# A two-block transformer kernel on one core: first tokens multiplied during the norm of the second, tokens stationary in the first block after each norm and in the gated layers, eight weight halves, the root in a diagonal tile

## The chip, the cores and the metric

The kernel runs on one core of one Trainium2 chip. The metric is device time in microseconds, the median of three runs: 1670.88 (1669.81 to 1671.94).

## The reference, cut to what matters

256 tokens of width 1024 pass through two blocks, everything in 32-bit floats. Each stage begins with an RMS norm over the whole width, so its first product needs the finished rows:

```python
h = h + concat(attn, rec) @ w_out            # after proj = rmsnorm(h) @ w_in      (mix1)
h = rmsnorm(h + peer(rmsnorm(h, norm2_g)))   # 2048-wide queries, top-16 keys, 16384 experts
# second block, two layers (even, odd), sh/sc/g from c @ ada_w + ada_b
hm = modulate(rms_norm(x, mix_norm), sh_m, sc_m)
x  = x + g_m * (mixer(hm) @ w_out)           # even: convolutions and a gated recurrence; odd: attention
hf = modulate(rms_norm(x, ffn_norm), sh_f, sc_f)
x  = x + g_f * ((silu(hf @ w_gate) * (hf @ w_up)) @ w_down)     # 2816 hidden columns
```

There are six norms that feed a product: before mix1, peer, even, the gated layer of even (here ffn0), odd, and the gated layer of odd (ffn1). The norm that closes the first block and the one that opens even are done in one pass.

## The kernel before, in words

Tokens lie in two groups of 128 (t = 0 and 1). Precision is kept by writing every operand as a sum of two parts, hi and lo; each product is three matmuls (hi hi, lo hi, hi lo).

**Weights** come as a stream of 1 MB units (`stream_init`, `load`, `unit`). One unit is fetched into one of two raw buffers by a DMA on SP's queue, and each of its halves (128 x 1024) is split: ScalarE (ACT) copies hi (L163), VectorE (DVE) subtracts lo (L166; some units on GpSimd). There are three buffers of halves (`SPB`, L364), and `unit` loads one unit ahead (`LA`, L149).

**Products** take two forms. `wstat` (L186) has the weights stationary and 256 token columns moving: 24 matmuls for 128 output columns, the output lies with columns on partitions. `xstat` (L200) has 128 tokens stationary and 512 weight columns moving. `out_n` (L218) uses it for products 1024 wide, with four accumulators [t][c] in PSUM; the last three steps of k (`TAIL`) are ordered by t and column group, so the first tokens end first. `out_n512` (L237) is the same for 512 columns, both token groups in turn.

**A norm** (`norm_t`, L304) runs per token group: add the four accumulators of the stage before to the residual (`add_res`, with a gate row multiplied in where there is one), squares (half on ACT, half on DVE), a root by Newton steps on DVE (`rsqrt1`, eight instructions on one column), scaling of the row by it (L332, L334), eight transposes on TensorE (PE, L338), gain and shift per column (L345 to L352, half on ACT, half on DVE), and the split of the result into hi and lo (L355, L356). The stage's first `wstat` needs both token groups.

**Gate rows** (`grow`, L949) lay a modulation column out along the free axis: 8 diagonal tiles on DVE, 8 fp32 matmuls with ones (16 instructions), two copies. The modulation itself (`ada_steps`) is 48 steps on DVE per layer, spread over pv and over even with ffn0.

**Order.** A planner lays out each engine's queue in advance: the program's order is the priority, an instruction that the planner's cost table does not hold for ready is passed by later ones, and `issue_after` pins one behind another on its engine. At run time each queue is in order.

The gated layer (`ffn`, L964) takes 22 steps, each with two `wstat` (gate, up), a Silu on ACT, a multiply on DVE and the split of the result. Names of the stages by their weights: wp and wo (mix1), wq, pu, pv (peer), wi0, wo0, fgu0, fd0, wi1, wo1, fgu1, fd1.

Of the kernel before, what the change touches and what calls it, by code (L numbers as in the profile page):

```python
# [18 lines left out]
D = 1024  # L19
# [69 lines left out]
def layout(i):  # L89
# [6 lines left out]
        _wcols(w, 2048, 4), _wcols(w, 1536, 4), qk[0:2], _wrows(w, 1024, 512),  # L96
        qk[2:4], _wrows(w, 2560, 512), _wrows(w, 3072, 512)], axis=0)
    a["wo"] = _wrows(g("w_out")[0])
    a["wq"] = _wcols(g("peer_wq")[0], 0, 16)
# [5 lines left out]
    for l in "01":  # L105
        a["ada" + l] = g(f"l{l}_ada_w_2").T.reshape(48, 128, 1024)
        a["fgu" + l] = _wpair(g(f"l{l}_ffn_w_gate_2"), g(f"l{l}_ffn_w_up_2"), 0, 0, 22)
# [3 lines left out]
    a["wi0"] = np.concatenate([_wcols(w, 2048, 4), _wcols(w, 512, 8), _wcols(w, 0, 4), _wcols(w, 1536, 4)], axis=0)  # L111
# [23 lines left out]
class Prog:  # L135
# [4 lines left out]
    def stream_init(self):  # L140
        order = []
        for nm in ("wp", "wo", "wq", "pu", "pv", "wi0", "wo0", "fgu0", "fd0", "wi1", "wo1", "fgu1", "fd1"):
            order.extend((nm, j) for j in range(self.i[nm].shape[0]))
# [5 lines left out]
    LA = 1  # L149

    POOLED = {"wq": (2, 8), "pu": (0, 6)}

    def load(self, n):
# [5 lines left out]
        for h in range(2):  # L159
            s = r[:, h * 1024:(h + 1) * 1024]  # L160
            hi = self.wp.tile([128, 1024], F32R, name="hi", bufs=self.SPB)
            lo = self.wp.tile([128, 1024], F32R, name="lo", bufs=self.SPB)
            nc.scalar.copy(hi, s)  # L163
            a, b = self.POOLED.get(nm, (0, 0))
            eng = nc.gpsimd if a <= j < b else nc.vector
            ins = eng.tensor_tensor(lo, s, hi.bitcast(F32), op=ALU.subtract)  # L166
# [19 lines left out]
    def wstat(self, half, x, K=8):  # L186
# [4 lines left out]
        pt = self.pt([128, 256])  # L191
        for k in range(K):
            c = slice(k * 128, k * 128 + 128)
            nc.tensor.matmul(pt, hi[:, c], xh[:, k], start=k == 0, stop=False)  # L194
            nc.tensor.matmul(pt, hi[:, c], xl[:, k], start=False, stop=False)  # L195
        for k in range(K):
            nc.tensor.matmul(pt, lo[:, k * 128:k * 128 + 128], xh[:, k], start=False, stop=k == K - 1)  # L197
        return pt

    def xstat(self, acc, half, x, k, first, last, cg, ts=(0, 1)):  # L200
# [3 lines left out]
        for t in ts:  # L204
# [4 lines left out]
            for c, cs in cg:  # L209
# [3 lines left out]
                nc.tensor.matmul(a, xl, hi[:, cs], start=False, stop=last)  # L213

    TAIL = 3
# [21 lines left out]
    def out_n512(self, nm, j0, x, lead=0, step=None):  # L237

        acc = [[self.acc([128, 512])] for t in range(2)]
        us = []  # L240

        def part(k, t):
# [3 lines left out]
            self.xstat(acc, us[k // 4][k // 2 % 2], x, k, k == 0, k == 7, [(0, slice(o, o + 512))], ts=(t,))  # L246

        for k in range(8 + lead):
            if k < 8:
                part(k, 0)  # L250
            if k >= lead:
                part(k - lead, 1)
# [1013 lines left out]
```

## Time and profile before

| | us |
|---|---|
| median of the runs | 1670.88 |
| the profiled execution | 1669.5 |
| its span | 1667.4 |
| PE busy | 1588.8 |
| DVE busy | 1272.1 |
| ACT busy | 863.0 |
| mean granted TensorE clock | 0.981 |

A matmul's shown duration holds its latency; what one costs in a stream is the distance from one start to the next. "x8" is eight instructions merged into one row. A wait is put down to the releaser that came last. In the windows the share of the clock is that of 2.4 GHz, so 0.5 is the lower of its two levels.

### The profile page before, as it was taken

To read this page: it belongs to the slowest core of one execution; us is meant where nothing else is said; L and a number is where in the kernel's file an instruction comes from. 1 tells how busy PE (TensorE), PEld (TensorE's weight loads), DVE (VectorE), ACT (ScalarE), POOL (GpSimd) and SP (SyncE) were. 2 spreads that over 40 slices of the span, in tenths; PEclk is the share of its full clock that TensorE was granted. 3 is DMA by queue.
4 is the path that set the end of the run, shared out by engine and by line. 5 is a ranking of instruction groups with operands and counts; after the bars stand their busy time and mean duration, and the time that the engine had idled before them with its cause. 6 is when DMAs were issued, how large, how long until landed. Compare 5 with 4: busy or idle time off the path is not lost.

```text
span 1667.4 us, 27542 instructions
## 1 busy us (share of the span) xinstructions
PE 1588.8 (95%) x10454; PEld 1448.1 (87%) x10454; DVE 1272.1 (76%) x2944; ACT 863.0 (52%) x1515; POOL 86.1 (5%) x47
## 2 busy tenths in 40 slices
PE   6998998999999999999999996989999799979998
PEld 6886898999999999888888886979998687779997
DVE  6967489868889897787777788967887877665544
ACT  6544445445444444555555555645444467654442
POOL 0310462000000000000000000000000000000000
PEclk9999899999999999999999998999999899989999
DMA  5324343544444444877777774656888453235554
GB/s 206 127 102 152 132 172 127 203 169 143 147 149 153 152 153 162 285 284 262 260 273 261 273 261 156 219 181 237 324 317 296 165 184 116 87 116 188 177 180 149
DMA packets 52405, 320.97 MB, mean 192 GB/s; under 512 B 5808, under 2 KB 6192, under 8 KB 20144
## 3 DMA queue, kind: packets, MB, share of 16 engines
q1 hardware_dynamic: 51264, 315.75, 53.8%
q10 hardware_dynamic: 1008, 3.47, 0.6%
q8 instruction: 81, 1.33, 0.3%
q14 instruction: 52, 0.43, 0.1%
HBM read 318.15 MB, written 1.05 MB: 191 GB/s over the span
## 4 chain that ended last, share of the span: by engine, by line
PE 88%; DVE 8%; ACT 1%; DMA 1%; issue 1%; POOL 0%; DVEq 0%; ACTq 0%
PE pt L194 15%; PE pt L195 15%; PE pt L197 15%; PE acc L211 12%; PE acc L212 12%; PE acc L213 12%; PE acc L829 3%; DVE lo L166 2%; PE pt L491 1%; PE pt L338 1%; PE pt L1166 1%; ACT hi L163 1%; DMA cr<-in_rows 0%; DVE xn L300 0%; PE acc L688 0%
## 5 line engine op out<-in xcount | busy, mean ns | idle before, releaser
L166 DVE TENSOR_TENSOR lo<-raw,hi 128x1024 fp32r<-128x1024 f32 x476 | 582.4, 1225 | 271.5 <-ACT hi L163 265.0
L163 ACT CAST hi<-raw 128x1024 fp32r<-128x1024 f32 x500 | 524.5, 1050 | 482.8 <-PE pt L195 231.7
L194 PE MATMUL pt<-xh,hi 128*128 128x256 f32 x2144 | 537.2, 288 | 9.7 <-ACT xh L355 8.8
L195 PE MATMUL pt<-xl,hi 128*128 128x256 f32 x2144 | 529.5, 285 | 0.6 <-DVE xl L356 0.6
L194 PEld LDWEIGHTS pt<-xh,hi 128*128 128x128 f32 x2144 | 411.9, 193 | 12.3 <-ACT xh L355 10.0
L195 PEld LDWEIGHTS pt<-xl,hi 128*128 128x128 f32 x2144 | 412.2, 192 | 1.3 <-DVE xl L356 1.1
L197 PE MATMUL pt<-xh,lo 128*128 128x256 f32 x2144 | 302.2, 284 | 5.1 <-DVE lo L166 4.4
L197 PEld LDWEIGHTS pt<-xh,lo 128*128 128x128 f32 x2144 | 277.0, 192 | 5.8 <-DVE lo L166 4.6
L212 PE MATMUL acc<-lo,wh 128*128 128x512 f32 x512 | 199.3, 389 | 0.6 <-DVE lo L166 0.6
L211 PE MATMUL acc<-hi,wh 128*128 128x512 f32 x512 | 199.2, 389 | 0.0
L213 PE MATMUL acc<-hi,wl 128*128 128x512 f32 x512 | 199.2, 389 | 0.0
L938 DVE SCALAR_TENSOR_TENSOR araw<-araw,sc 128x1024 f32<-128x1024 f32 x96 | 116.1, 1218 | 0.0
L212 PEld LDWEIGHTS acc<-lo,wh 128*128 128x128 f32 x512 | 96.1, 188 | 20.8 <-DVE lo L166 1.0
L213 PEld LDWEIGHTS acc<-hi,wl 128*128 128x128 f32 x512 | 96.1, 188 | 20.1
L211 PEld LDWEIGHTS acc<-hi,wh 128*128 128x128 f32 x512 | 96.1, 188 | 19.9
L827 DVE TENSOR_SCALAR B<-iota,idxT,idxT 128x128 f32<-128x128 f32 x256 | 86.8, 339 | 0.0
L212 PE MATMUL acc<-lo,yh 128*128 128x512 f32 x208 | 81.5, 392 | 0.0
L213 PE MATMUL acc<-hi,yl 128*128 128x512 f32 x208 | 81.2, 390 | 0.0
L211 PE MATMUL acc<-hi,yh 128*128 128x512 f32 x208 | 80.8, 391 | 0.0
L258 ACT CAST wh<-actB 128x128 fp32r<-128x128 f32 x176 | 48.8, 297 | 57.7 <-PE acc L212 53.7
L338 PE MATMUL pt<-ident,xn 128*128 128x128 f32 x96 | 22.0, 412 | 53.1 <-DVE xn L334 52.6
L837 ACT COPY actB<-acc 128x352 f32<-128x352 f32 (+31 forms) x64 | 20.2, 316 | 100.5 <-DVE actB L835 97.1
(295 smaller groups left out, 1882.4 us busy)
## 6 DMA issues: line engine op xcount, KB each, us to landing
raw<-in_pu SPq DMA_DIRECT2D x64, 1024.0 KB, 4.9
raw<-in_pv SPq DMA_DIRECT2D x64, 1024.0 KB, 4.9
araw<-in_ada SPq DMA_DIRECT2D x96, 512.0 KB, 5.6
raw<-in_fgu SPq DMA_DIRECT2D x44, 1024.0 KB, 4.9
raw<-in_wi SPq DMA_DIRECT2D x22, 1024.0 KB, 4.9
raw<-in_fd SPq DMA_DIRECT2D x22, 1024.0 KB, 4.9
raw<-in_wp SPq DMA_DIRECT2D x14, 1024.0 KB, 4.9
raw<-in_wo SPq DMA_DIRECT2D x12, 1024.0 KB, 4.9
```

The source lines that it names most:

```text
L163: nc.scalar.copy(hi, s)
L166: ins = eng.tensor_tensor(lo, s, hi.bitcast(F32), op=ALU.subtract)
L194: nc.tensor.matmul(pt, hi[:, c], xh[:, k], start=k == 0, stop=False)
L195: nc.tensor.matmul(pt, hi[:, c], xl[:, k], start=False, stop=False)
L197: nc.tensor.matmul(pt, lo[:, k * 128:k * 128 + 128], xh[:, k], start=False, stop=k == K - 1)
L211: nc.tensor.matmul(a, xh, hi[:, cs], start=first, stop=False)
L212: nc.tensor.matmul(a, xh, lo[:, cs], start=False, stop=False)
L213: nc.tensor.matmul(a, xl, hi[:, cs], start=False, stop=last)
L258: self.nc.scalar.copy(hi, src)
L827: nc.vector.tensor_scalar(B, iota, idxT[1][:, t:t + 1], idxT[2][:, t:t + 1], op0=ALU.is_equal, op1=ALU.mult)
L829: nc.tensor.matmul(gp[:, n], A, B, start=True, stop=True)
L938: nc.vector.scalar_tensor_tensor(w, w, 1.0, self.sc, op0=ALU.mult, op1=ALU.mult, accum_out=m[:, k:k + 1])
```

## The change

1. `norm_t` computes token group 0 wholly, then `ahead` issues that group's 24 matmuls of the next stage's first 512 columns, while group 1 is normed; group 1's diagonal matmuls are pinned behind the sixth of the eight k steps (`mark`). The two units that `ahead` needs are already loaded; loads after it are pinned behind the norm's last split (`after`).
2. The row is no longer scaled by its root. The root goes into a diagonal tile (`dr`), and a plain fp32 matmul of the row with it does transpose and scaling at once. All squares and all gains are ACT's.
3. The first 512 columns of wp, wq and wi0 are computed with tokens stationary and turned by 8 transposes (`turned`); all of fgu0 and fgu1 so, in 11 blocks of 256 gate and 256 up columns, with 4 transposes of the gated product per block.
4. Eight buffers of halves (5 more in a second pool, `ext`) and two units ahead, except in the second half of pu and most of pv. pv runs its second part first, so that the memory for it can be freed.
5. Gate rows go out to device memory as columns (1024 pieces of 4 bytes) and come back as a row spread over the partitions; `grow` is gone.
6. `TAIL` is 4, and pv's tail is ordered by column group too.

```diff
+    RAWB = 2
+    SPB = 3
+    EXT = 5
+    def roomy(self, n):
+        nm, j = self.order[n]
+        return self.ext is not None and not (nm == "pu" and j >= self.JT // 2)
     def load(self, n):
...
+            with ExitStack() as es:
+                for i in self.after:
+                    es.enter_context(self.tc.issue_after(i))
+                nc.scalar.copy(hi, s)
+                ins = eng.tensor_tensor(lo, s, hi.bitcast(F32), op=ALU.subtract)
     def unit(self, nm, j):
-        while self.nload <= min(n + self.LA, len(self.order) - 1):
+        while self.nload < len(self.order) and self.nload <= n + (2 if self.roomy(self.nload) else 1):
-    TAIL = 3
+    TAIL = 4
-    def out_n512(self, nm, j0, x, lead=0, step=None):
+    def out_n512(self, nm, j0, x, first=None, step=None):
+        us, acc = first or ([], [[self.acc([128, 512])], None])
+        acc[1] = [self.acc([128, 512])]
+        for k in range(8):
...
+            for t in (1,) if first else (0, 1):
+                self.xstat(acc, us[k // 4][k // 2 % 2], x, k, k == 0, k == 7, [(0, slice(o, o + 512))], ts=(t,))
+    def ahead(self, nm, j0, x):
+        us = [self.ready.pop(self.pos[(nm, j0 + n)]) for n in range(2)]
+        acc = [[self.acc([128, 512])], None]
+        for k in range(8):
+            o = (k % 2) * 512
+            ins = self.xstat(acc, us[k // 4][k // 2 % 2], x, k, k == 0, k == 7, [(0, slice(o, o + 512))], ts=(0,))
+            if k == 5:
+                self.mark = ins.ins
+        return us, acc
+    def turned(self, nm, j0, x, first, st):
+        a01 = self.out_n512(nm, j0, x, first)
+        for t in range(2):
+            nc.scalar.copy(st[:, t], a01[t])
+        for c in range(4):
+            pt = self.pt([128, 256])
+            for t in range(2):
+                nc.tensor.transpose(pt[:, t * 128:t * 128 + 128], st[:, t, c * 128:c * 128 + 128], self.ident)
+            yield pt
     # norm_t, per token group t
-                a, b = self.mean2(tp, ht, xn)
+                for c in range(2):
+                    if self.left:
+                        with self.tc.issue_after(dr_ins) if t and c else ExitStack():
+                            self.add_res(t, c)
+                    ms.append(self.square(tp, ht[:, cs]))
+                    if row is not None:
+                        nc.vector.tensor_tensor(src[:, cs], ht[:, cs], row[:, cs], op=ALU.mult)
+                        ms.append(self.square(tp, src[:, cs]))
                 r = self.rsqrt1(tp, m)
+                dr = tp.tile([128, 128], F32, name="dr", bufs=2)
+                dr_ins = nc.vector.tensor_scalar(dr, self.ident, r, None, op0=ALU.mult).ins
                 for g in range(2):
-                    if g:
-                        nc.scalar.activation(xn[:, gs], ht[:, gs], AF.Copy, scale=r)
-                    else:
-                        nc.vector.tensor_scalar(xn[:, gs], ht[:, gs], r, None, op0=ALU.mult)
-                        nc.tensor.transpose(pt[:, k], xn[:, o:o + 128], self.ident)
+                    with self.tc.issue_after(self.mark) if t else ExitStack():
+                        for k in range(4):
+                            nc.tensor.matmul(pt[:, k], src[:, o:o + 128], dr, start=True, stop=True)
+                    for k in range(4):
+                        nc.scalar.activation(y[:, k], pt[:, k], AF.Copy if shift is None else AF.Identity, ...)
+                    c_ins = nc.scalar.copy(xhs, y)
+                    v_ins = nc.vector.tensor_tensor(xls, y, xhs.bitcast(F32), op=ALU.subtract)
+                if t == 0:
+                    first = self.ahead(nm, 0, (xh, xl))
+        self.after = (c_ins.ins, v_ins.ins)
     # peer, pv
-                for j in range(64):
+                for n, j in enumerate(list(range(JT // 2, 64)) + list(range(JT // 2))):
...
+                    for cg in self.CG:
+                        for half, w in tail:
+                            self.xstat(acc, half, w, None, False, half is tail[-1][0], [cg], ts=(t,))
     # ada_steps: gate columns out; row(): back as a row
+                with self.tc.issue_after(self.last_load.ins):
+                    nc.sync.dma_start(self.kept[l, g].rearrange("o (k p) -> p (o k)", p=128), m)
+        r = self.rp.tile([128, 1024], F32, name="g", bufs=1)
+        self.nc.sync.dma_start(r, self.kept[l, n].broadcast_to([128, 1024]))
     # ffn
-        for m in range(22):
-            u = self.unit(f"fgu{l}", m)
-            p0 = self.wstat(u[0], x)
-            p1 = self.wstat(u[1], x)
-            nc.scalar.activation(sg, p0, AF.Silu)
-            nc.vector.tensor_tensor(y, sg, p1, op=ALU.mult)
-            self.split(yh[:, m], yl[:, m], y)
+        for b in range(11):
+            a01 = self.out_n512(f"fgu{l}", 2 * b, x, None if b else first)
+            pt = self.pt([128, 2, 256])
+            for t in range(2):
+                y = p.tile([128, 256], F32, name="fy", bufs=4)
+                nc.scalar.activation(y, a01[t][:, 0:256], AF.Silu)
+                nc.vector.tensor_tensor(y, y, a01[t][:, 256:512], op=ALU.mult)
+                for c in range(2):
+                    nc.tensor.transpose(pt[:, c, t * 128:t * 128 + 128], y[:, c * 128:c * 128 + 128], self.ident)
+            self.split(yh[:, 2 * b:2 * b + 2], yl[:, 2 * b:2 * b + 2], pt)
```

## Rows read from the trace of the kernel before

**Rows 1.** The page, busy time of each engine: us (share of the span) xinstructions.

```profile
PE 1588.8 (95%) x10454; PEld 1448.1 (87%) x10454; DVE 1272.1 (76%) x2944; ACT 863.0 (52%) x1515; POOL 86.1 (5%) x47
```

**Rows 2.** Waits of PE: line, releaser, us in total, times, longest.

```profile
PE pt L338 <- DVE xn L334: 52.6, 9, 9.1
...
PE pt L197 <- DVE lo L166: 4.4, 1, 4.4
```

**Rows 3.** Windows at the six norms: us, busy by engine, clock, DMA.

```profile
0.00:17.50 17.50, 3.50 (x16) 3.17 (x16) 11.30 (x45) 11.81 (x25) 2.69 (x7) 0.95 0.64 249
17.50:23.60 6.10, 5.69 (x28) 5.40 (x29) 2.72 (x8) 2.06 (x5) 0.00 (x0) 0.59 0.52 172
159.80:172.60 12.80, 3.26 (x17) 2.41 (x16) 10.21 (x27) 7.29 (x17) 0.00 (x0) 0.74 0.24 83
172.60:176.30 3.70, 3.63 (x17) 3.62 (x18) 1.39 (x2) 0.91 (x3) 0.00 (x0) 0.52 0.31 58
1011.60:1031.10 19.50, 6.58 (x33) 5.70 (x32) 18.74 (x72) 10.00 (x21) 0.00 (x0) 0.65 0.36 135
...
1115.80:1129.80 14.00, 6.90 (x33) 6.23 (x32) 12.28 (x35) 8.81 (x18) 0.00 (x0) 0.63 0.22 77
1317.10:1329.50 12.40, 3.77 (x18) 3.14 (x17) 11.83 (x43) 5.48 (x11) 0.00 (x0) 0.60 0.22 85
...
1459.60:1475.30 15.70, 6.28 (x33) 5.96 (x32) 13.85 (x41) 9.38 (x20) 0.00 (x0) 0.67 0.19 67
```

**Rows 4.** Timeline of DVE in ffn0's norm: start, length, line, tiles.

```profile
1115.68 2.36 DVE L166 TENSOR_TENSOR lo<-raw,hi 128x1024 fp32r<-128x1024 f32 x2 [0.17 <-ACT hi L163]
...
1121.69 0.15 DVE L264 TENSOR_SCALAR r<-m 128x1 int32<-128x1 int32 x1
...
1123.54 0.49 DVE L334 TENSOR_SCALAR xn<-h,r 128x512 f32<-128x512 f32 x1
```

**Rows 5.** By source line, the norm's operations: ns min/median/max, first and last start.

```profile
L299 ACT ACTIVATE xn<-h x14: 614/630/635, 5.3 to 1463.5; 128x512 f32<-128x512 f32 x14
L299 ACT ACTIVATION_READ_ACCUMULATOR xn<-h x14: 185/187/188, 5.9 to 1464.0; 128x1 f32 x14
...
L958 DVE TENSOR_SCALAR dg<-ident,modc x32: 271/278/318, 833.3 to 1335.5; 128x128 f32<-128x128 f32 x32
...
L349 ACT ACTIVATE y<-pt,modc,modg x32: 447/457/490, 1021.5 to 1475.6; 128x128 f32<-128x128 f32 x32
...
L355 ACT CAST xh<-y x24: 607/618/651, 13.2 to 1476.2; 128x512 fp32r<-128x512 f32 x24
...
L356 DVE TENSOR_TENSOR xl<-y,xh x24: 674/692/694, 13.9 to 1476.8; 128x512 fp32r<-128x512 f32 x24
```

**Rows 6.** Timeline of PE, four places at full clock.

```profile
304.95 1.12 PE L197 MATMUL pt<-xh,lo 128*128 128x256 f32 x8
...
307.83 1.12 PE L197 MATMUL pt<-xh,lo 128*128 128x256 f32 x8
...
352.31 1.06 PE L829 MATMUL acc<-B,A 128*128 128x128 f32 x8
...
1352.22 1.03 PE L1155 MATMUL pt<-ident,qn 128*128 128x128 f32 x8
```

**Rows 7.** Windows in pv, in fgu0 and in odd.

```profile
676.00:1004.00 328.00, 328.00 (x1449) 271.57 (x1448) 259.45 (x479) 183.81 (x367) 0.00 (x0) 1.00 0.76 269
1130.00:1264.00 134.00, 134.00 (x1087) 132.56 (x1087) 109.90 (x165) 65.88 (x94) 0.00 (x0) 1.00 0.84 304
1340.00:1440.00 100.00, 99.91 (x478) 76.76 (x478) 74.66 (x180) 70.02 (x114) 0.00 (x0) 1.00 0.39 135
```

**Rows 8.** By source line, the gated product in ffn.

```profile
L981 ACT ACTIVATE fsg<-pt x44: 372/378/386, 1135.6 to 1599.9; 128x256 f32<-128x256 f32 x44
...
L982 DVE TENSOR_TENSOR fy<-fsg,pt x44: 412/421/423, 1136.6 to 1602.8; 128x256 f32<-128x256 f32 x44
```

**Rows 9.** The page's DMA queues: packets, MB, share of 16 engines.

```profile
q1 hardware_dynamic: 51264, 315.75, 53.8%
```

More of the change, by code (lines that the diff above doesn't have):

```diff
@@ L142, in stream_init @@
         for nm in ("wp", "wo", "wq", "pu", "pv", "wi0", "wo0", "fgu0", "fd0", "wi1", "wo1", "fgu1", "fd1"):
-            order.extend((nm, j) for j in range(self.i[nm].shape[0]))
+            js = list(range(self.i[nm].shape[0]))
+            if nm == "pv":
+                js = js[self.JT // 2:] + js[:self.JT // 2]
+            order.extend((nm, j) for j in js)
         self.order = order
@@ L212, in xstat @@
                 nc.tensor.matmul(a, xh, lo[:, cs], start=False, stop=False)
-                nc.tensor.matmul(a, xl, hi[:, cs], start=False, stop=last)
-    TAIL = 3
+                ins = nc.tensor.matmul(a, xl, hi[:, cs], start=False, stop=last)
+        return ins
+    TAIL = 4
     CG = [(0, slice(0, 512)), (1, slice(512, 1024))]
@@ L366, in run, with x_tiles, square @@
+        self.after = (c_ins.ins, v_ins.ins)
+        self.last_lo = v_ins
+        return (xh, xl), first
+    def x_tiles(self, pool):
+        return tuple(pool.tile([128, 8, 256], F32R, name=n, tag=n, bufs=1) for n in ("xh", "xl"))
+    def square(self, pool, h):
+        a = pool.tile([128, 1], F32, name="m2", bufs=8)
+        jk = pool.tile([128, 512], F32, name="jk", bufs=2)
+        self.nc.scalar.activation(jk, h, AF.Square, scale=D ** -0.5, accum_out=a)
+        return a
     def run(self):
@@ L429, in mix1 @@
         cum = p.tile([128, 4, 256], F32, name="cum")
-        for hd in range(4):
-            if hd % 2 == 0:
-                u = self.unit("wp", hd // 2)
+        st = p.tile([128, 4, 256], F32, name="xx", bufs=3)
+        for hd, pt in enumerate(self.turned("wp", 0, x, first, st.rearrange("p a b -> p (a b)").rearrange("p (t n) -> p t n", t=2))):
             if hd == 0:
@@ L786, in peer @@
             hst = halves()
+            ahead = self.turned("wq", 0, x, first, p2.tile([128, 2, 512], F32, name="qst", tag="oh", bufs=1))
             for c in range(16):
-                if c % 2 == 0:
-                    u = self.unit("wq", c // 2)
-                pt = self.wstat(u[c % 2], x)
+                if c < 4:
+                    pt = next(ahead)
+                else:
+                    if c % 2 == 0:
+                        u = self.unit("wq", c // 2)
+                    pt = self.wstat(u[c % 2], x)
                 qps[c] = p3.tile([128, 256], F32, name="qp", bufs=3)
@@ L946, in ada_steps @@
                                                op0=ALU.add, op1=ALU.mult)
[L947 to L961 removed]
+            if n in (2, 5):
+                due.append((n, m))
+            if n < 5:
+                yield
+        send()
+        yield
     def ffn(self, l, st=iter(()), final=False):
@@ L989, in ffn @@
             pass
-        self.left = (acc, grow, p, final)
+        self.left = (acc, self.rows[l, 5], p, final)
         if final:
             for t in range(2):
-                self.add_res(t)
+                for c in range(2):
+                    self.add_res(t, c)
             es.close()
```

260 lines of the change are left out of this document (131 added, 129 removed).

## The prediction

> **What bounds the kernel now.** I read the busy times first: PE is busy 1588.8 of 1667.4 us, so only 79 us are idle there [rows 1]; what PE streams in the other time is bought back only by a cheaper form of the same product. Next the waits of PE: 52.6 of the 79 us are nine waits of the norm's transposes for the scaled row, and the one large wait elsewhere is 4.4 us for a lo half, in pu while DVE sorts [rows 2]. Then windows laid from the last matmul of one stage to the first weight matmul of the next: 17.5, 12.8, 19.5, 14.0, 12.4 and 15.7 us, together 91.9, in which PE does nothing but transposes and gate rows, and its clock falls (0.60 to 0.74 in the later five; a mean of the levels 1.2 and 2.4 GHz) [rows 3]. After two of them the first weight matmuls still run slow: 6.1 us at 0.59 for 24 matmuls that take 2.88 at full clock (worked out below), 3.2 lost, and 3.7 us at 0.52, 1.8 lost [rows 3]. So the six norms cost 91.9 + 5.0 = 97 us. Last, what fills a norm: DVE is busy 12.3 of ffn0's 14.0 us, and a part of that is not the norm at all: lo halves for the next stage (2.36 us for two, inside the chain) [rows 3, 4].
>
> **The norm, step by step, on ffn0.** Let E be the end of the last matmul before it. A 512-column matmul costs 328/1449 = 0.226 us in a stream [rows 7]; with four k steps in the tail the accumulators end at E-8.1, E-5.4, E-2.7 and E, twelve matmuls apart. Group 0: the second accumulator is multiplied by the gate and added (two DVE passes of 128x512, 0.69 each as L356), ready at E-4.0; its square and the read-out 0.82 on ACT, E-3.2; the root from its first instruction to its user 1.85 (1121.69 to 1123.54), E-1.3; with group 1's third accumulator between (1.4) E+0.1; the diagonal 0.28 [rows 4, 5]. A plain fp32 matmul is two instructions; eight in 1.06 us [rows 6], so group 0's first four columns are out at E+1.5. ACT now has all four gains (0.46 each) and the cast (0.62): E+3.9, the second four E+6.4, lo by DVE at E+7.0 [rows 5]. From E+3.9 PE does the 24 matmuls of group 0; mark falls at about E+8.7. Group 1: the last accumulator is in the row by E+1.6, its square stands behind group 0's gains on ACT (E+7.2), root and diagonal to E+9.3, matmuls, gains and cast to E+12.9, where group 1's 24 matmuls start. Since 24 x 0.226 = 5.4 us of useful work are done by then, the norm costs 12.9 - 5.4 = 7.5; if the square slips in before the gains, mark is what holds, and it is 5. I take 6.8, near the sum step by step. The queue behind the new pins: loads wait behind the last split, on ACT and DVE; they are two units on, which PE needs only 5.4 us later, so I cost that at nothing; without that cover it is one lo pair, 2.4.
>
> For norm2, odd and ffn1 I use the same 6.8 (norm2 has no gate and no shift, somewhat less). Even has a multiply and two squares more per group: 8.4. In mix1's norm ACT is busy 11.8 of 17.5 us already [rows 3] and gets gains and two units' casts more, so group 1 starts some 5 us later than the first matmul now, 22.5, less 5.4: 17; bounds 13 and 21. Sum after: 17 + 4 x 6.8 + 8.4 = 53 against 97: 44 less. Each hop between engines that I priced at nothing and the planner's misjudgements I set at 4: **40 less**. Bounds: all five at 5, 52 less; and if the clock stays at the lower level through the first tokens' matmuls, each norm loses what norm2's does now, 1.8 to 3: 28 less.
>
> **The other parts.** Gate rows: four blocks of 16 instructions; those of even, ffn0 and ffn1 lie inside the windows above, the one before wo1 stands in a full stream: 2 x 1.06 = 2 us less [rows 6]. Their return by DMA is needed a stage later, cost nothing (its rival below).
>
> Form of the product: 128 columns with weights stationary take 2.88 us (304.95 to 307.83, 24 matmuls, 0.120 each), so four take 11.52; the same 512 columns with tokens stationary 48 x 0.226 = 10.87 [rows 6, 7]. 0.65 less per block; but transposes are 0.13 each (1.03 for eight) [rows 6]: 0.52 per gated block, 1.03 for a turned one. Each visit to transposes may also cost a change-over, not shown apart: 0 to 0.2. Gated layers: 22 x (0.65 - 0.52 - 0.1) = 0.7 less, bounds 3 less and 4 more; I write 0. Three turned blocks: 3 x 0.4 = 1 more.
>
> The Trainium skill has another price for that. "TensorE: Matmul & The Clock Gate", Back-to-back issue gap, has the columns divided by 2.4 GHz plus 2.5 ns, that is 109 and 216 ns, and so saves only 2.5 ns for each pair of short matmuls merged. By it the gated layers would come out about 22 x 0.5 = 11 us slower than by my rows. The rows show 120 and 226 ns, a fixed part of 13 ns; they decide, and a total of 1637 by the page gets no chance of its own.
>
> Eight halves: the waits for halves in pu (4.4 us [rows 2], and the half clock behind it) go as far as one unit more (5.8 us of PE) covers a DVE that is full there; I take 5 less, bounds 2 and 7. TAIL in pv holds 16 of 16 w tiles; the last half's tiles wait for the step before: 0 to 2, 1 more. DVE in fgu0 is at 110 of 134 [rows 7]; the new form takes two multiplies and one wide split for four narrow passes, no more than before.
>
> **Sum**, on the profiled execution's own 1669.5: -40 - 2 + 0 + 1 - 5 + 1 = -45, so 1624.5; the runs' median lies 1.4 above the profiled one: **1626**.
>
> **Rivals.** *The shadow is only half used.* Group 0's matmuls run at the lower clock, or ACT, with all squares, gains and casts (4 x 2.45 us and 4 x 0.82 in one norm), is late for both groups, and PE idles in two pieces in place of one. For it: the clock falls in all six windows now. Against it: the new idle pieces are under 4 us, where the present ones reach 9.1 [rows 2], and plain matmuls fill them. Then the norms give 20 and the rest 3: 1648.
>
> *Gate rows hold up the weights.* The skill's "DMA: Bandwidth & Descriptors", Specifications, says that pieces below 512 bytes make the engine read, modify and write; a gate row goes out in pieces of 4. No run here shows such a piece. From rows: a packet now takes 0.538 x 16 x 1667/51264 = 0.28 us [rows 9]; 1024 as dear, over 16 engines, are 18 us of all queues for each of four rows. In pv a quarter is free; in fgu0 DMA is at 0.84, 21 us of 134 free [rows 7], and two units ahead cover 11 us. Worst case some 7 us lost for two of them: 1641.
>
> *The transposes of the gated blocks stop PE* (the slower side). They stand in PE's queue behind a Silu (0.38 each, two) and a multiply (0.42) [rows 8] that start only when the block's matmuls are through: 1.2 us with drain and transposes about 1.9, and 2.9 where the Silu stands behind a weight cast and the multiply behind a lo. If the planner leaves them at the block's end, 22 x 2.9 = 64 us more: 1690. It decides from 45/22 = 2.0 us per block on. For it: PE's queue is in order at run time. Against it: in odd, with transposes and attention steps of just this kind among its matmuls, PE idles 0.09 of 100 us [rows 7]; the planner passes them by.
>
> **Chances.** Forecast 0.64 (its own range 1606 to 1640), half shadow 0.19, gate rows 0.09, gated blocks slower 0.08. A measurement of this kernel tells 0.2% (3.3 us) from no change. Faster 0.91, same 0.02, slower 0.07 (the slower rival in a mild form is no change). The range of 8 in 10 reaches from 1604 (norms 52, gated layers 3, halves 7, no cost in pv) to 1654 (half shadow with some loss in the gated layers).
>
> **What would show it.** Right: between two stages PE idle in pieces below 4 us, with 24 matmuls of 512 columns before group 1's diagonal matmuls; windows like those of rows 3 with the clock near 1; no wait over 2 us for a lo half in pu; fgu0's blocks 11.4 us apart. Wrong: idle pieces over 6 us in the norms with ACT full; blocks of fgu0 13 us apart; waits of hi casts for weight DMAs in fgu0. The prediction is wrong if the time is above 1654, above all if the norms shrink as told and the time does not.

## The result and the profile after

The changed kernel takes 1689.8 us (median of four runs, 1683.5 to 1691.1) against 1670.9: ratio 1.0106, 95% interval 1.0079 to 1.0132. It is 1.1% slower; 1626 was forecast. The page and the waits of PE, as [rows 1] and [rows 2] had them (busy us by engine; then line, releaser, us in total, times, longest):

```profile
PE 1601.1 (95%) x9398; PEld 1398.9 (83%) x9398; DVE 1233.9 (73%) x2816; ACT 863.3 (51%) x1555; POOL 83.6 (5%) x47
```

```profile
PE pt L397 <- DVE dr L389: 29.1, 4, 11.4
PE acc L241 <- ACT xh L404: 15.8, 12, 2.2
PE acc L241 <- ACT hi L193: 9.6, 2, 4.9
```

The nine waits for the scaled row, 52.6 us, are now four for the diagonal tile and twelve for hi of x, 44.9 together. Waits of PE for hi halves of weights were 1.5 us in three before and are now 9.6 in two. The six norms, in windows from the last matmul of a stage to the second group's first matmul, beside [rows 3] (us, busy by engine, clock, DMA share, GB/s):

```profile
0.00:25.81 25.81, 14.36 (x57) 11.81 (x57) 9.62 (x28) 14.87 (x34) 0.20 (x4) 1.00 0.57 210
163.47:176.35 12.88, 10.54 (x62) 8.55 (x60) 3.80 (x14) 6.46 (x20) 0.00 (x0) 1.00 0.00 0
1021.60:1047.41 25.81, 11.84 (x58) 9.78 (x56) 14.97 (x54) 14.69 (x36) 0.00 (x0) 0.74 0.35 128
1127.50:1146.99 19.49, 13.34 (x58) 11.15 (x56) 7.16 (x27) 8.41 (x24) 0.00 (x0) 0.74 0.16 61
1340.90:1361.37 20.47, 11.83 (x59) 9.78 (x57) 11.94 (x41) 12.10 (x27) 1.28 (x4) 0.83 0.60 138
1483.90:1501.74 17.84, 12.39 (x57) 10.22 (x56) 6.93 (x27) 8.23 (x23) 0.00 (x0) 0.81 0.07 30
```

They sum to 122.3 us. In each the first group's 24 matmuls are done, 5.45 us of useful work at full clock; taking 6 x 5.45 off leaves 89.6 where the forecast had 53 and the kernel before had 97 (91.9 and 5.0 of slow matmuls behind). So the shadow (the first group's matmuls inside the norm) is there, and yet the norms hardly became cheaper.

The larger loss lies elsewhere. In pv, PE stands for 5 us at a place where it did not stand before. First PE's timeline there (start, length, line, tiles, idle before and its releaser), then the DMA view of 850 to 874, whose GB/s row has slices of 0.6 us:

```profile
868.02 0.39 PE L243 MATMUL acc<-hi,wl 128*128 128x512 f32 x1
873.27 0.50 PE L241 MATMUL acc<-hi,wh 128*128 128x512 f32 x1 [4.86 <-ACT hi L193]
```

```profile
GB/s 273 55 41 27 150 123 246 437 423 375 389 410 75 42 177 0 0 0 0 82 27 14 41 55 14 27 27 0 27 14 41 205 355 382 410 437 423 416 410 416
...
raw<-in_pv SPq DMA_DIRECT2D x3, 1024.0 KB, 12.0
araw<-in_ada SPq DMA_DIRECT2D x2, 512.0 KB, 9.0
row<-modc SPq DMA_DIRECT2D x1, 4.0 KB, 15.2
```

The last line is a gate row's write, issued at 852.6: 4 KB take 15.2 us to land, and the 1 MB units beside it 12.0 where the page's median for in_pv is 5.6. In the GB/s row the reader sees sixteen slices, 9.6 us (859.0 to 868.6), at 0 to 82 GB/s between stretches at 400, the first four of them empty. The pieces themselves do not fill them, as the DMA view of 857.0 to 858.1 and then that of 858.1 to 868.7 shows:

```profile
DMA packets 1085, 0.12 MB, mean 112 GB/s; under 512 B 1056, under 2 KB 1056, under 8 KB 1085
```

```profile
DMA packets 45, 0.37 MB, mean 35 GB/s; under 512 B 0, under 2 KB 0, under 8 KB 0
q1 hardware_dynamic: 45, 0.37, 100.2%
```

The pieces are booked within 1.1 us. In the 10.6 us behind them only 45 packets of the weights were started, and they count as busy for the time of all 16 engines, some 3.8 us each (10.6 x 16 / 45), where a packet of the kernel before takes 0.28 by [rows 9]. What is slow is the weights' transfer, until the write has landed.

Another write stands at pv's end. This is ACT's timeline in front of even's norm, and one line of DVE's:

```profile
1013.83 2.00 ACT L193 CAST hi<-raw 128x1024 fp32r<-128x1024 f32 x2 [3.22 <-DMA raw<-in_wi]
1025.54 1.99 ACT L193 CAST hi<-raw 128x1024 fp32r<-128x1024 f32 x2 [9.70 <-DMA raw<-in_wi]
1027.43 0.63 ACT L423 ACTIVATE jk<-h 128x512 f32<-128x512 f32 x1
```

```profile
1018.39 0.68 DVE L373 TENSOR_TENSOR hf<-h,gf 128x512 f32<-128x512 f32 x1
```

The second write was issued at 1010.5, the second unit of wi0 behind it at 1011.6. That unit is late, and its casts stand in ACT's queue ahead of the norm's squares (L423). Their row was there at 1019.1 and they start at 1027.4: ACT idles 9.70 us for a weight that the squares do not need, and PE 11.4 us for the diagonal tile. The list of the change says that the two units which `ahead` needs are already loaded; here the second of them is not. The third write (1229.5) makes fgu0 stop for 4.7 us.

By stage, from the starts of the first and last weight matmuls in each trace (us; "512 B", "no shadow" and "best" are experiments below):

| | before | after | 512 B | 512 B, no shadow | best |
|---|---|---|---|---|---|
| mix1 | 159.4 | 163.5 | 164.8 | 155.7 | 155.2 |
| peer up to pv | 503.1 | 496.3 | 495.9 | 492.2 | 493.1 |
| pv | 348.9 | 361.8 | 350.7 | 349.6 | 349.6 |
| even with its norm | 104.1 | 105.9 | 97.3 | 100.4 | 95.3 |
| ffn0 with its norm | 201.3 | 213.4 | 202.9 | 210.8 | 200.6 |
| odd with its norm | 142.5 | 143.0 | 139.8 | 139.5 | 137.8 |
| ffn1 with its norm | 203.1 | 198.4 | 197.1 | 201.1 | 196.2 |

Any edit makes the planner lay out every queue anew, so single cells move by some us for reasons that are not the edit's; the verdicts below go by whole times.

### The profile page after: what moved, and what is told of

It reads as the page before. It is cut to its first block, busy times and chain, and to the rows that moved or that the text cites. A ratio compares the mean times of both kernels' runs of the same rounds, so it can differ in the third digit from the quotient of the medians.

```text
span 1687.1 us, 25219 instructions
## 1 busy us (share of the span) xinstructions
PE 1601.1 (95%) x9398; PEld 1398.9 (83%) x9398; DVE 1233.9 (73%) x2816; ACT 863.3 (51%) x1555; POOL 83.6 (5%) x47
## 3 DMA queue, kind: packets, MB, share of 16 engines
HBM read 320.24 MB, written 1.06 MB: 190 GB/s over the span
## 4 chain that ended last, share of the span: by engine, by line
PE 65%; DVE 14%; DMA 12%; ACT 4%; issue 4%; POOL 1%; SPq 0%; ACTq 0%; DVEq 0%; POOLq 0%
PE acc L241 12%; PE acc L242 12%; PE acc L243 12%; PE pt L224 7%; PE pt L225 7%; PE pt L227 7%; DVE lo L194 5%; PE acc L909 3%; DMA raw<-in_fgu 3%; DMA raw<-in_fd 2%; ACT hi L193 2%; DVE araw L1041 2%; DMA raw<-in_pv 2%; DMA raw<-in_wi 2%; PE pt L397 1%
## 5 line engine op out<-in xcount | busy, mean ns | idle before, releaser
L224 PE MATMUL pt<-xh,hi 128*128 128x256 f32 x1344 | 338.2, 289 | 3.2 <-ACT actA L923 1.6
L225 PE MATMUL pt<-xl,hi 128*128 128x256 f32 x1344 | 330.7, 284 | 0.0
L224 PEld LDWEIGHTS pt<-xh,hi 128*128 128x128 f32 x1344 | 257.9, 192 | 4.4 <-ACT actA L923 1.8
L225 PEld LDWEIGHTS pt<-xl,hi 128*128 128x128 f32 x1344 | 258.4, 192 | 0.1
L241 PE MATMUL acc<-hi,xh 128*128 128x512 f32 x544 | 219.7, 404 | 20.4 <-ACT xh L404 15.8
L242 PE MATMUL acc<-lo,xh 128*128 128x512 f32 x544 | 217.7, 400 | 0.8 <-DVE lo L194 0.8
L243 PE MATMUL acc<-hi,xl 128*128 128x512 f32 x544 | 217.6, 400 | 0.2 <-DVE xl L405 0.2
L227 PE MATMUL pt<-xh,lo 128*128 128x256 f32 x1344 | 189.1, 283 | 0.0
L241 PEld LDWEIGHTS acc<-hi,xh 128*128 128x128 f32 x544 | 104.4, 192 | 44.7 <-ACT xh L404 18.6
L242 PEld LDWEIGHTS acc<-lo,xh 128*128 128x128 f32 x544 | 104.5, 192 | 21.4 <-DVE lo L194 1.1
```

Source lines behind the costliest of these rows:

```text
L224: nc.tensor.matmul(out, hi[:, c], xh[:, k, ts], start=k == 0, stop=False)
L225: nc.tensor.matmul(out, hi[:, c], xl[:, k, ts], start=False, stop=False)
L227: nc.tensor.matmul(out, lo[:, k * 128:k * 128 + 128], xh[:, k, ts], start=False, stop=k == K - 1)
L241: nc.tensor.matmul(a, xh, hi[:, cs], start=first, stop=False)
L242: nc.tensor.matmul(a, xh, lo[:, cs], start=False, stop=False)
L243: ins = nc.tensor.matmul(a, xl, hi[:, cs], start=False, stop=last)
```

## The experiments

Ratios are to the kernel before, run on the same chip beside each; its medians lay at 1669.4 to 1670.4.

**The gate rows.** Theory 1: the writes hold up the weights.

```diff
 a1_no_write: in send()
-                with self.tc.issue_after(self.last_load.ins):
-                    nc.sync.dma_start(self.kept[l, g].rearrange("o (k p) -> p (o k)", p=128), m)
+                pass
 in row()
-        self.nc.sync.dma_start(r, self.kept[l, n].broadcast_to([128, 1024]))
+        self.nc.sync.dma_start(r, self.i["rows"][:, 1536:2560].broadcast_to([128, 1024]))
```

> The changed kernel without its four writes of gate rows to DRAM (4 KB each, in pieces of 4 bytes): the rows are read back from an input of the same size instead, so the gates are other numbers and the output is not the reference's. Theory 1, the writes hold up the weights behind them (stalls read in the changed kernel: 5.0 and 1.0 us in pv, some 10 at the end of pv and in even's norm, 7 in fgu0): 1690 less 15 to 22, so 1668 to 1675, and no wait of a hi cast for raw over 2 us left on PE's path at these places. Rival, those stalls come from SP issuing two units ahead behind tiles that are not free yet: 1685 to 1691.

Measured: 1659.2 (ratio 0.9920, 0.9906 to 0.9934), 31 us less than the changed kernel, by the medians and by the ratios, more than theory 1 had set. pv is back at 350.3, fgu0 has no stop.

```diff
 a2_write512: in send()
+                pt = self.pt([8, 128])
+                nc.tensor.transpose(pt, m, self.ident)
+                mt = spare[0].tile([128, 256], F32, name=spare[1], bufs=2)[0:8, 0:128]
+                nc.scalar.copy(mt, pt)
                 with self.tc.issue_after(self.last_load.ins):
-                    nc.sync.dma_start(self.kept[l, g].rearrange("o (k p) -> p (o k)", p=128), m)
+                    nc.sync.dma_start(self.kept[l, g].rearrange("o (k p) -> (o k) p", p=128), mt)
```

> The changed kernel with the gate rows still written to DRAM and read back, but turned first by one PE transpose and an ACT copy to 8 partitions of 128, so that each write is 8 pieces of 512 bytes and not 1024 of 4. Theory 1 (the number of pieces is the price): within 4 us of the kernel without the writes, so 1668 to 1678, and a write lands in under 5 us instead of 14.5. Rival (any write in this queue costs it, a wait for the value or for the round trip): 1684 to 1691, like the changed kernel.

Measured: 1658.4 (0.9933, 0.9919 to 0.9946): the same as with no write at all. The same bytes at the same places, in 8 pieces for 1024, cost nothing that can be seen. The write's landing is not in the trace; the DMA view from 858 to 882 shows none of the low stretch after its issue at 864.5 (the eleventh slice):

```profile
GB/s 137 150 328 423 423 287 0 0 0 109 164 328 423 437 341 315 389 116 7 150 246 437 437 416 300 328 280 55 164 232 369 423 423 246 307 348 109 191 314 410
```

```diff
 b1_write_act: in send()
-                    nc.sync.dma_start(self.kept[l, g].rearrange("o (k p) -> p (o k)", p=128), m)
+                    nc.scalar.dma_start(self.kept[l, g].rearrange("o (k p) -> p (o k)", p=128), m)
```

> The changed kernel with its four 4-byte-piece writes of gate rows issued by ACT's DMA queue and not by SP's, which carries the weights. If a write costs because the weights stand behind it in one queue: 1658 to 1668, near the kernel without writes (1659). If its 1024 pieces occupy the DMA engines that the weights need, whichever queue they come from: 1682 to 1692, like the changed kernel.

Measured: 1681.4 (1.0075, 1.0049 to 1.0101), 8 less than the changed kernel by the medians, 5 by the ratios, whose intervals overlap, and 23 more than with 512-byte pieces. The DMA view from 827 to 851, the write issued at 829.6:

```profile
GB/s 314 369 102 109 205 273 410 410 362 294 430 135 152 68 0 0 0 68 27 27 41 41 27 14 27 14 14 55 14 410 423 396 382 444 444 396 423 410 389 376
```

Again sixteen slices, 9.6 us, at 0 to 68 GB/s, though the write comes from another queue. So the write holds back the weights' transfers from whichever queue it comes; that taking it out of their queue gains anything is not shown. By 9.6 us x 16 engines / 1024, a piece costs some 0.15 us of an engine (an estimate).

The Trainium skill's "DMA: Bandwidth & Descriptors", Specifications, wants pieces of at least 512 bytes and says that smaller ones are read, modified and written. The runs agree in direction: 4-byte pieces cost 29 to 31 us, 512-byte pieces nothing that can be seen. What an engine does in the slow stretch, and so whether it reads and rewrites there, no run here shows.

```diff
 b4_before_writes: the kernel before, in ada_steps
+                if k == 3:
+                    send()      # four writes as the changed kernel does them; nobody reads them
```

> The kernel before with nothing of the change but four writes of the gate columns to DRAM as the changed kernel does them (4 KB in 4-byte pieces, on SP's queue, three steps after the value); nothing reads them, the gate rows are still made by PE. Theory 1 (a write holds up the weights by some 10 us and one unit ahead covers 5): 20 to 35 slower, 1690 to 1705. If the price exists only with the changed kernel's two units ahead or its read back: 1670 to 1676.

Measured: 1683.6 (1.0086, 1.0073 to 1.0099), 14 us for the four writes alone: below what theory 1 gave, far above the rival. A write costs 3.4 us there and some 7.5 in the changed kernel (29 to 31 over four). In the kernel before, pv is 6.0 longer with them and even with its norm 5.7. Why the changed kernel pays double was not tried.

**The shadow.**

```diff
 a3_no_shadow: in norm_t
-                    with self.tc.issue_after(self.mark) if t else ExitStack():
-                        for k in range(4): ...
+                    for k in range(4): self.mark = nc.tensor.matmul(...).ins
-                if t == 0:
-                    first = self.ahead(nm, 0, (xh, xl))
+        with self.tc.issue_after(self.mark):      # after both groups
+            first = self.ahead(nm, 0, (xh, xl))
```

> The changed kernel with the first tokens' 24 matmuls held back until the second tokens' diagonal matmuls have been issued, at all six norms: nothing of the product lies in the norm any more. If the shadow hides all of the 24 matmuls (5.4 us at full clock, as the prediction had it): 32 us slower, 1722. If it hides about half (late first group, half clock): 10 to 20 slower, 1700 to 1710. If it is worth nothing: 1687 to 1693.

Measured: 1678.3 (1.0043, 1.0029 to 1.0056): 11 faster than with the shadow, which none of the three lines had. mix1 gained 8.2, ffn0 6.2, odd lost 5.4. Since the writes' stops move about, this run can't be read as the shadow's worth; so it was repeated on the kernel with 512-byte writes.

```diff
 d1_pieces_no_shadow = a2_write512 with the edit of a3_no_shadow
```

> The changed kernel with gate rows written in 512-byte pieces (1658) and with the first tokens' 24 matmuls held back until the second tokens' diagonals are issued: the worth of the shadow itself, without weights that come late. If it hides what the forecast counted (5.4 us in each of five norms and part of it in the first): 25 to 30 slower, 1683 to 1688. If what it hides is given back by the second group's diagonals and gains, which stand behind all 24 matmuls (1.67 and 1.8 us, PE idle), and by the first norm, where both groups could start at once: 1655 to 1663.

Measured: 1659.4 (0.9942, 0.9929 to 0.9956) against 0.9933: the shadow, as ordered, is worth about nothing. By windows, from a stage's end to the next stream's first matmul, the six norms take 14.6, 6.4, 14.7, 15.6, 12.4 and 15.6 us without the shadow, together 79.3, and 72.2 with it (5.45 each taken off): in the five later norms the shadow wins 12, in mix1's it loses 5. There both groups' rows are in memory at the start, and without the pin behind the sixth k step (`mark`) all 48 matmuls run from 14.6 on; with it the second group starts at 24.7. The stages say the same: even and ffn1 are 3 and 4 longer without the shadow, mix1 9 and the peer's front (peer up to pv) 4 shorter. Only 5 of mix1's 9 and 1 of the front's 4 lie in their norms; where the rest comes from is not shown. ffn0 of this run also holds a wait of 5.6 us for a turned gate row (1.2 in the other), so without that the shadow would look worse still, not better.

**The gated layers' form.**

```diff
 a4_gated_wstat: in ffn, blocks 1 to 10 as before the change
+                for m in (2 * b, 2 * b + 1):
+                    u = self.unit(f"fgu{l}", m)
+                    p0 = self.wstat(u[0], x)
+                    p1 = self.wstat(u[1], x)
+                    ...
```

> The changed kernel with blocks 1 to 10 of both gated layers as before the change (weights stationary, 256 columns, no transposes); block 0, which the norm's first tokens need, stays as it is. From the stretches of ffn1, where no weights are late (125.6 us with tokens stationary, 127.2 with weights stationary), tokens stationary saves 1.6 per layer: 1690 to 1694. Rival (the transposes and the wide split cost the layers what the forecast feared): 1670 to 1684. In fgu0 the stall behind the write stays in both.

Measured: 1686.2 (1.0102, 1.0086 to 1.0117) against 1.0106: no difference, and by the median between the two ranges that were set. Windows over the same part of fgu1, tokens stationary in the changed kernel, then weights stationary in this one:

```profile
1501.74:1621.94 120.20, 120.13 (x544) 97.06 (x545) 72.10 (x80) 63.54 (x83) 0.00 (x0) 1.00 0.56 197
```

```profile
1496.13:1617.60 121.47, 121.47 (x988) 120.11 (x989) 72.48 (x90) 67.12 (x95) 0.00 (x0) 1.00 0.56 199
```

1.3 us less for the new form over ten blocks, with PE full in both: in fgu1 the gated product's transposes do not stop it. In fgu0, where DVE has the modulation to do as well, PE waits for them a little (line, releaser, us in total, times, longest, in the changed kernel):

```profile
PE pt L1076 <- DVE fy L1074: 3.5, 4, 1.4
```

**The order inside a norm.** Theory 2: the second group's chain stands behind the first group's gains, and its diagonals behind all 24 matmuls. From the kernel with 512-byte writes, ffn0, stage end at 1108.68: PE, then ACT and DVE (start, length, line, operation):

```profile
1111.19 2.05 PE L397 MATMUL pt<-dr,h 128*128 128x128 f32 x16 [2.12 <-DVE dr L389]
1114.80 0.50 PE L241 MATMUL acc<-hi,xh 128*128 128x512 f32 x1 [1.56 <-ACT xh L404]
...
1120.66 1.95 PE L397 MATMUL pt<-dr,h 128*128 128x128 f32 x16
1124.17 0.50 PE L241 MATMUL acc<-hi,xh 128*128 128x512 f32 x1 [1.56 <-ACT xh L404]
```

```profile
1112.39 1.85 ACT L400 ACTIVATE y<-pt,modc,modg 128x128 f32<-128x128 f32 x5 [1.98 <-PE pt L397]
...
1115.66 0.67 ACT L423 ACTIVATE jk<-h 128x512 f32<-128x512 f32 x1
```

```profile
1102.54 2.36 DVE L194 TENSOR_TENSOR lo<-raw,hi 128x1024 fp32r<-128x1024 f32 x2 [3.36 <-ACT hi L193]
1104.81 1.28 DVE L720 TENSOR_TENSOR gy<-acc,g 128x512 f32<-128x512 f32 x2
...
1110.85 0.29 DVE L389 TENSOR_SCALAR dr<-ident,r 128x128 f32<-128x128 f32 x1
...
1118.73 0.29 DVE L389 TENSOR_SCALAR dr<-ident,r 128x128 f32<-128x128 f32 x1
```

The last square runs at 1115.66, behind eight gains and one cast, though its row was ready at 1112.46; the diagonals wait until all 24 are through, and then PE idles 1.56 for the gains.

```diff
 b2_between = a2_write512; in norm_t both groups' adds, squares, roots and diagonal tiles first, then
+            for t in range(2):
+                src, dr = all_src[t], drs[t]
                 ... diagonals, gains, split
                 if t == 0:
-                    first = self.ahead(nm, 0, (xh, xl))      # 8 k steps
+                    first = self.ahead(nm, 0, (xh, xl))      # 3 k steps, 9 matmuls
+                if t and g:      # behind the second group's diagonals: the other 15
+                    with self.tc.issue_after(dg):
+                        self.ahead_rest(first, (xh, xl))
```

> The kernel with gate rows in 512-byte pieces (1658), with the norm in another order: both groups' squares and roots come ahead of the first group's gains, and the second group's diagonal matmuls stand after 9 of the first group's 24 matmuls, the other 15 behind them (before: after all 24, where PE then idles 1.56 us for the second group's gains). Theory 2 (the norms fall short because group 1's chain stands behind group 0's gains on ACT and its diagonals behind all 24 matmuls; read in ffn0: diagonal tile ready 10.3 us after the stage's end, second group's first matmul at 15.5): 2 to 3 us less per norm, 1640 to 1648. Rival (the first group's late start and the lower clock set it, the order does not matter): 1655 to 1661.

Measured: 1646.9 (0.9874, 0.9858 to 0.9890), 10 us less by the ratios, inside theory 2's range at its weak end. But half of it is mix1 (159.1 for 164.8), whose norm became only 0.7 shorter. Measured on PE's timeline from the start of a stage's last matmul to the start of the last of the 48 matmuls for the next 512 columns, the six norms take 139.6 us in sum with 512-byte writes and 135.1 reordered. So, by one trace each, at most 4.5 of the 10 are theory 2's; the rest lies outside the norms, and its cause is not shown. In ffn0 nothing came: the windows there show why (from the diagonals to the second diagonals; clock third from the end):

```profile
1101.00:1103.10 2.10, 2.10 (x16) 2.10 (x16) 1.19 (x2) 0.95 (x3) 0.00 (x0) 0.83 0.24 92
1103.10:1105.20 2.10, 0.39 (x3) 0.09 (x2) 1.36 (x8) 2.10 (x7) 0.00 (x0) 0.50 0.41 158
1105.20:1109.30 4.10, 4.10 (x9) 2.85 (x10) 1.74 (x4) 1.60 (x4) 0.00 (x0) 0.51 0.00 0
```

After waits of 2.1 and 1.7 us the granted clock is 0.5, and the nine matmuls take 3.9 us from the first start to the last, 1.8 at full clock. What the order won in ffn0, the clock took.

```diff
 b3_between_split = b2_between, with the gains shared as before the change
+                        if k % 2: nc.scalar.activation(y[:, k], ...)
+                        else: nc.vector.tensor_scalar(y[:, k], ...)
```

> As the run beside it, and the gains are shared between DVE and ACT, two columns of four each, as they were before the change. If ACT's gains in series (four of 0.35 to 0.46 us ahead of each cast) are part of what is late: some 0.8 us per cast, 1 to 2 us less per norm than the run beside it, 1630 to 1642. If not: the same as the run beside it within 3 us.

Measured: 1651.2 (0.9884, 0.9866 to 0.9901): the same. Sharing ACT's gains brings the time nothing.

**The clock.** Theory 3: the waits themselves slow what comes after them.

```diff
 c1_warm = b2_between
+    def keep(self, n, after):      # n plain matmuls of a tile of ones, chained behind `after`
+        pt = self.pt([128, 128])
+        ...
+            warm = None if nm == "wq" else self.keep(10 if self.left else 14, self.last_mm)
+                    with self.tc.issue_after(self.keep(6, dg)):
                         first = self.ahead(nm, 0, (xh, xl))
```

> The reordered norm with 512-byte gate writes (1647), and PE kept busy where it waits in a norm by plain matmuls of a tile of ones that nothing reads: 10 between the stage's last matmul and the first diagonal matmul (14 before the first norm, none in the second), 6 between the first group's diagonals and its first weight matmul. Theory 3 (after 2 us of idle the granted clock is 0.5 for the diagonals and for all nine first weight matmuls: 3.9 us for 9 in ffn0, 2.04 at full clock, and 2.1 to 3.4 us for diagonals that take 1.67): 1.8 to 3.5 less per norm, 10 to 16 in all, 1631 to 1637. Rival (the clock follows its own course, or the wait for the scaled tile only gets longer by what PE gains): 1643 to 1650; the extra matmuls in the way of the diagonals cost at most 0.2 us each time.

Measured: 1636.1 (0.9801, 0.9786 to 0.9816), 12 less by the ratios, as theory 3 had it. The sum over the six norms falls from 135.1 to 123.2, so here the whole gain lies in the norms. ffn0's norm there:

```profile
1097.67 2.39 PE L288 MATMUL pt<-ones 128*128 128x128 f32 x20
1100.47 2.05 PE L418 MATMUL pt<-dr,h 128*128 128x128 f32 x16 [0.41 <-DVE dr L408]
1102.36 1.50 PE L288 MATMUL pt<-ones 128*128 128x128 f32 x12
1104.86 0.50 PE L242 MATMUL acc<-hi,xh 128*128 128x512 f32 x1 [0.99 <-ACT xh L428]
...
1107.31 1.95 PE L418 MATMUL pt<-dr,h 128*128 128x128 f32 x16
```

From the first of the nine matmuls to the second diagonals it is now 2.45 us (1104.86 to 1107.31), where it was 4.19 (1105.18 to 1109.37).

```diff
 d2_pieces_warm = a2_write512 with the same extra matmuls, in the changed kernel's own order
```

> The changed kernel with 512-byte gate writes (1658), in its own order, with the same extra matmuls of a tile of ones in the norms' waits (10, 6, 14 in the first): the clock's part without the other order. By the rows of that kernel: diagonals 1.67 us at full clock took 3.34, 2.45, 1.78, 2.42 and 2.82, first 24 matmuls 5.6 took 7.4, 7.2 and 7.2 in three norms; together some 10: 1647 to 1650. If the clock's price comes only with the other order: 1655 to 1660.

Measured: 1652.9 (0.9898, 0.9883 to 0.9913), 6 less than 0.9933, of the 10 set. The order alone gives 10, the clock alone 6, both 22. In the six norms of the traces the order alone gives 4.5, the extra matmuls alone 1.4, both 16.4: most of the 6 lies outside the norms too, and only together do the two shorten the norms by much. I read it so (not tried apart): with the clock held, the diagonals come early enough to hide the gains.

```diff
 d3_before_warm: the kernel before, extra matmuls of the same kind in its norms' waits
+                if self.fills[t]:
+                    warm = self.keep(self.fills[t], dg if t else self.last_mm)
```

> The kernel before, with nothing of the change, and plain matmuls of a tile of ones in its norms' waits (14, then 30 between the two halves of the second norm, 34 and 20, 28, 36, 36). If the clock after idle time cost the kernel before too (transposes and gate rows at half speed, first weight matmuls 5.0 us): 5 to 10 faster, 1660 to 1665. If the waits grow by what PE gains, or the extra matmuls stand in the way: 1668 to 1675.

Measured: 1669.6 (0.9996, 0.9987 to 1.0005): nothing. Windows in ffn0 and ffn1 of this run, for 0.63 and 0.67 in [rows 3]:

```profile
1115.80:1129.80 14.00, 10.53 (x90) 9.87 (x88) 12.08 (x35) 9.19 (x20) 0.00 (x0) 1.00 0.23 77
1459.10:1473.50 14.40, 12.86 (x107) 11.83 (x105) 13.73 (x41) 8.67 (x19) 0.00 (x0) 1.00 0.20 73
```

The clock is full, and yet ffn0's norm is as long as before, ffn1's 1.6 shorter: DVE is busy for 12.1 of the 14.0 and 13.7 of the 14.4 us and, as I read it, sets the end, so a faster PE mostly waits longer. The 5 us that the forecast booked as the clock's cost in the kernel before were not to be had: behind mix1's norm the first weight matmul starts 1.3 earlier (16.3 for 17.5), and the 124th starts at 34.9 as before (35.0).

**The best kernel.** The turned gate rows whose value comes last make PE wait, as the waits of b2_between show:

```profile
PE pt L1040 <- DVE modc L1063: 4.7, 2, 3.2
```

```diff
 c3_late = b2_between; c2_warm_late = c1_warm; both with the last write of each layer one stage later
-        send()
+        self.flush = send      # called in even and in odd
```

> The reordered norm with 512-byte gate writes (1647), the last two writes one stage later, without the extra matmuls: 4 to 5 less, 1641 to 1643. If fd0's length (65.9 us against 59.9 in the kernel before) comes from something else than that transpose: 1645 to 1648.

> As the run beside it, and the two gate rows whose value is the last of its modulation pass are turned and written one stage later (in even and in odd), so that their transposes do not stand in PE's queue waiting for DVE (read in the reordered kernel: 3.2 us in fd0 and 1.4 at the end of pv): 4 to 5 less than the run beside it, about 1627 to 1632 if theory 3 holds.

Measured: c3_late 1645.0 (0.9862, 0.9847 to 0.9877) against 0.9874, c2_warm_late 1634.7 (0.9797, 0.9784 to 0.9811) against 0.9801: within the intervals, no gain shown of the 4 to 5 set. The wait is gone, fd0 is 62.4 for 65.9, but odd's norm and fgu0 took it back. c2_warm_late beats both kernels: 2.0% faster than before. Its page, and the window of ffn0's norm:

```profile
PE 1599.0 (98%) x9582; PEld 1406.6 (86%) x9582; DVE 1230.4 (75%) x2816; ACT 863.6 (53%) x1559; POOL 81.4 (5%) x47
```

```profile
1093.30:1103.33 10.03, 9.81 (x76) 8.84 (x74) 5.58 (x20) 6.10 (x16) 0.00 (x0) 1.00 0.15 52
```

## Why the prediction was wrong

**The step that failed first: "their return by DMA is needed a stage later, cost nothing".** It cost 31 us of the 64 by which the forecast missed (1689.8 to 1658.4 by the size of the pieces alone; 29 by the ratios). The rival for it, with chance 0.09, pointed at the right place, and its price for a write, some 7 us, is near the 7 to 8 measured. But it counted two of the four writes (1641), and the price came out by luck, from two errors that cancel. It put 18 us of all queues on a write, which was too much (9.6 us of low rate, some 0.15 us a piece against 0.28), and then let "two units ahead cover 11 us", where they covered some 2: a write cost most of its 9.6. A late unit does not only stop its own matmuls: its casts wait in ACT's queue, and at a stage's end the norm's squares stand behind them (9.70 us in even).

**The step that failed next: the norms, 97 to 53.** Without writes they stand at 72.2, so 25 were won and not 40 to 44. By norm, forecast and measured with 512-byte writes: mix1 17 and 19.3, norm2 6.8 and 7.4, even 8.4 and 11.9, ffn0 6.8 and 10.0, odd 6.8 and 12.0, ffn1 6.8 and 11.5. In ffn0 the working, step by step: the diagonal tile was set for 0.4 after the end and came at 2.5. A pair of lo halves (2.36 us at 1102.54) stands ahead of the gate's multiply, and both halves of the row are multiplied before either is added (1104.81 to 1107.29), so the row is ready 1.4 before the end and not 4.0; the adds between the root's steps were in the forecast. Gains began at 3.7 for 1.5, the first group at 6.1 for 3.9, the second at 15.5 for 12.9. The shape was right, the start 2.2 late and the end 2.6. The lower bound of 5 does not come out of the prediction's own steps: with `mark` at E+8.7, 1.06 of matmuls and 2.46 of gains and cast, the second group starts at E+12.2, which costs 6.8. In even, odd and ffn1 the half clock adds to it (granted 0.80, 0.80 and 0.90 over those norms; diagonals 2.4 to 2.8 for 1.67, 24 matmuls 7.2 for 5.6 in even and odd). The rival "the shadow is only half used", 1648, was nearest to what the kernel does without the writes (1658 to 1659).

**The shadow's credit.** By [rows 3] the forecast took 5.4 us of useful work in each norm as won. d1 shows that the time without it is the same: the rest of the change brings 12.6 in windows (91.9 to 79.3; the diagonal tile and the gate rows taken out of the norms, by my reading), the shadow 12 more in five norms. Mix1's norm, where the pin holds a second group back that could go at once, returns 5; mix1 and the peer's front return the other 7 outside their norms, for a cause that is not shown. The forecast had 17 for mix1's norm, near to its 17.5 before, and did not ask what the pin takes from a norm that has no stage before it.

**The slow first matmuls as a gain.** The forecast took the 5 us of slow matmuls behind norms as won. The change made new waits of 1.6 to 3 us between short bursts of PE, and behind some of them the clock is 0.5 (in ffn0 of b2_between above). Holding it up with matmuls of no use brought 6 us in the changed order, of which 1.4 in the norms, and 12 in the other, all of them there.

**Outside the norms.** There the forecast had 5 less (-2, 0, 1, -5, 1). With 512-byte writes the stages are 13.9 shorter in sum and the norms 24.8, so the rest became 10.9 longer: 16 of the 64, of which fd0 is 5.0 and pv 1.8; the others are not settled.

**Right.** Gated layers 0 (1.3 less in ffn1's ten blocks, 0 in the time). That is 0.13 a block, 0.65 less 0.52 as the rows gave; the 0.1 that the prediction adds for a change-over to transposes is shown by no run. Their transposes cost PE 3.5 us in fgu0 and nothing in fgu1, not 64, so the slower rival, 1690, met the time by chance and not by its mechanism. Eight halves: pu's wait of 4.4 us is gone, but the 5 less is not to be seen: the peer's front is 7.2 shorter with 512-byte writes, and its norm alone 7.2 (from 12.8 and 1.8 to 7.4). TAIL in pv: 1 forecast, a wait of 2.2 for a lo tile in the changed kernel, and pv 1.8 longer with 512-byte writes. What was named as a sign of failure, hi casts waiting for weight DMAs in fgu0, came (60.8 us of ACT's time, and 4.7 of PE's).

**Open.** fd0 of the kernels without write stops is 62 to 68 us for 59.9 before; moving the turned rows took 3.5 of it in b2_between, the rest is not settled. That mix1 moves by 3 to 5 us outside its norm between kernels whose edits lie in the norms is put down to the planner, and was not tried by itself. The eight halves, the three turned blocks, the tail of 4 and the diagonal tile were not taken out one at a time.

## What to carry to other kernels

A transfer is priced by its pieces before its bytes: before a column goes to memory as a row, turn it on the chip (one transpose and one copy here, for 29 to 31 us over four writes). When a wait is filled with useful work, ask what queues the filler stands in: work pinned in front of the second half's chain can delay it by as much as it saves, and a stage that had no wait only loses. In a stage made of short bursts, see at which clock the bursts run, and whether PE or another engine sets its end: only in the first case are idle matmuls worth their place.

## What the runs showed of the hardware

- 4 KB in 1024 pieces of 4 bytes took 14.5 us to land (median of four; 13.8 when added to the kernel before, 12.1 from ACT's queue). In pv of the changed kernel the pieces were booked within 1.1 us, and for 9.6 us behind them the sixteen DMA engines moved no more than 82 GB/s (68 with the write on ACT's queue); 1 MB takes 4.9.
- In ffn0 of b2_between PE idled 2.1 us before the diagonals and 1.7 behind them, and the granted clock was 0.5 over the next nine 512-column matmuls; with plain fp32 matmuls of 128 columns in the two waits (c2_warm_late) it was 1.00.
- Holding the clock full in the norms of the kernel before changed its time by nothing (ratio 0.9996).
